# Hybrid DeltaNet and dilated-attention block: one attention clump per step, and weights split anew for each token half

## The chip, the cores and the metric

The kernel runs on one core of a Trainium2 chip. The time is the device time of one execution in microseconds, taken as the median of several runs. Before the change it is 2402.37 us (three runs, 2398.69 to 2404.38). The engines are named as the profile names them: PE (TensorE; PEld are its weight loads), DVE (VectorE), ACT (ScalarE), POOL (GpSimd) and SP (SyncE), which here issues nearly all DMAs.

## The reference, cut to what matters

One decoder layer on 2048 tokens with 1024 channels, all in float32:

```python
h = rms_norm(x, norm_w)
proj = h @ w_in                                   # 1024 x 9224
(dn_qkv, dn_z, dn_b, dn_a, swa_q, swa_k, swa_v, swa_z, gates) = split(proj)
# A: gated DeltaNet, 4 heads: causal conv, silu, l2 norm, chunked delta rule, norm, silu gate
y_dn = o_dn @ w_branch_dn
# B: three groups (window, dilation) = (128,1), (512,4), (2048,16), 4 heads of 128 each:
sq, sk = partial_rope(rms_norm(swa_q)), partial_rope(rms_norm(swa_k))
o_g, lse_g = dilated_window_attention(sq[g], sk[g], sv[g])      # causal, dilated, softmax
o_swa = sum(softmax(lse) * o_g) * silu(swa_z)
y_swa = o_swa @ w_branch_swa
merged = sigmoid(g_dn) * y_dn + sigmoid(g_swa) * y_swa
x = x + merged @ w_out
```

## The kernel before, in words

Float32 products are made of three matmuls on split operands: a high part, cast by a copy on ACT, and a low part, raw minus high, by a subtraction on DVE or POOL (high x high, high x low, low x high).

The projections to q, k and v of branch B (and the two small DeltaNet columns) come first. The 2048 tokens stand in two halves of 1024, called p = 0 and p = 1. In each half a **first unit** makes the values of group 2 straight from x while x is normalised and split, and eight **units** follow. A unit multiplies 1024 tokens by 512 columns with Winograd's form of Strassen's scheme: seven products (the table `PROD`) on quarter operands and their sums S1 to S4 (of x) and T1 to T4 (of weights). Those of x are made once per half (`x_sums`, `x_put`). For a half of p = 0 the weights of each product are loaded raw (`w_load`), summed on DVE (`w_sums`, line 262), copied to the high part on ACT (`w_high`, line 283), and subtracted to the low part (`w_low`, line 290; T2, T3 and T4 on POOL, the others on DVE). Each split weight is then written to a scratch in DRAM (`park`, line 296), and the units of p = 1 read it back (`w_ahead`, line 311) in place of the raw one.

The order on PE, DVE, ACT and POOL is that of the program text; SP's order is the scheduler's. The program spreads work by **hooks**: after every six matmuls `hook()` counts one tick and emits whatever has come due; `at(delay, fn)` puts a function so many ticks ahead. So a delay sets where an instruction stands in its engine's queue, and an instruction that waits there holds all behind it.

**Attention** of a head and group is cut into items of 128 queries. An item runs through: load of q, k and v (`a_load`, lines 565, 566), transposes of q and k (`a_trans`, line 572) with their split into kq on ACT and DVE (579, 580; 576 for group 2), score (`a_score`, lines 590 to 592, or 587) with mask and minimum on DVE (594) and exp on ACT (598), transposes of p (`a_ptrans`, 605) with a copy on ACT (607), and the product with the values (`a_pv`, 613, 614), copied out on DVE (616) and written to scratch (619). One step of `att_loop` has three phases, each at a hook of its own: p's transposes; the score; then the values' product and the next item's transposes. A step takes four hooks in the first half and three in the second. What is left runs in the background of the units that follow.

After the attention projections come 36 **column units** (`cunits`, lines 717 to 719): 128 columns by 2048 tokens in four blocks, for gates and the DeltaNet's k, q and v. The first three are gates; then `open_dn` waits until attention is done and starts the chain of decay matrices E (`e_chain`: a load of gcb, a mask on POOL at line 850, `diff` on DVE at line 857, an exp on ACT). The k block's convolution runs on DVE (lines 823, 827, 832) and its result kT is transposed on PE (883). A scan over chunks, the branch products and the output projection follow; the change leaves them alone.

In the first unit each group of 128 tokens is read twice: by rows (`x_nat`, tile xt, one buffer) for the statistic (`x_stat`) and a diagonal matrix (`x_diag`, 149), and by channels (`x_chan`) for the values; a matmul with the diagonal (153) spreads the scale over the partitions. `x_plan` sets the ticks of all of these.

## Time and profile before

| | |
|---|---|
| median of the runs | 2402.37 us |
| the profiled execution | 2406.0 us, span 2404.2 us |
| PE busy | 2317.2 us, 96% of the span |
| DVE, ACT, POOL busy | 1345.1, 914.8, 886.5 us |
| granted TensorE clock, mean | 0.986 |
| HBM read, written | 263.45 MB, 185.89 MB |
| first unit of p = 0 | about 0 to 70 us |
| units of p = 0 | about 75 to 484 us |
| first unit of p = 1 | about 484 to 556 us |
| units of p = 1 | about 556 to 1015 us |
| column units | from about 1016 us |

PE is busy nearly all the time, so what matters are the gaps on PE and the stretches at a lower clock. A row of the waits gives the waiting instruction, whom it waited for, the sum in us, how often, and the longest.

### The profile page before, as it was taken

The page shows a single profiled execution, that of the slowest core. Times are in us where ns is not written, and L with a number is a line of the kernel's source. Part 1 is how long each engine was busy: PE and PEld are TensorE (multiplying, and loading weights), DVE is VectorE, ACT ScalarE, POOL GpSimd, SP SyncE. Part 2 cuts the span into 40 slices and gives each one's busy share as a digit, 9 for nine tenths or more (in the row PEclk, how much of TensorE's full clock was granted, in tenths as well). Part 3 has the DMA queues.
Part 4 walks back from the last instruction along what each step waited for, and adds up shares of the span by engine and source line. Part 5 has one row for each costly group of instructions (what it writes and reads, how often), then busy time and mean ns, then how long its engine had stood idle before and what let it go on. Part 6 is the DMA issues. An engine that isn't in the chain of part 4 may idle for free.

```text
span 2404.2 us, 43315 instructions
## 1 busy us (share of the span) xinstructions
PE 2317.2 (96%) x15218; PEld 2092.4 (87%) x15218; DVE 1345.1 (56%) x2854; ACT 914.8 (38%) x2941; POOL 886.5 (37%) x1330
## 2 busy tenths in 40 slices
PE   8999999989999999899999999999999999999999
PEld 7998998989999999877778888888888878889998
DVE  6465566675445545443877775999344433344431
ACT  5245455663324435433666662111233313111110
POOL 5263254575403303310845661102233222433441
PEclk9999999989999999999999999999999999999999
DMA  9988888877787787763445443222667645555442
GB/s 308 328 258 266 274 269 247 252 218 235 230 251 235 244 269 221 242 185 93 129 129 133 123 105 120 71 74 71 191 201 208 189 143 158 152 178 163 146 139 76
DMA packets 525968, 452.22 MB, mean 188 GB/s; under 512 B 66168, under 2 KB 490424, under 8 KB 523320
## 3 DMA queue, kind: packets, MB, share of 16 engines
q1 hardware_dynamic: 525464, 449.39, 61.4%
q8 instruction: 121, 1.98, 0.3%
q14 instruction: 95, 0.78, 0.1%
q10 hardware_dynamic: 288, 0.07, 0.0%
HBM read 263.45 MB, written 185.89 MB: 187 GB/s over the span
## 4 chain that ended last, share of the span: by engine, by line
PE 68%; DMA 10%; DVE 6%; issue 5%; POOL 5%; ACT 4%; SPq 1%; POOLq 0%; DVEq 0%; ACTq 0%
PE mm L422 17%; PE mm L717 9%; PE mm L718 9%; PE mm L719 9%; DMA qk<-qks 2%; PE mm L1247 2%; PE mm L1249 2%; PE mm L1248 2%; PE mm L1230 2%; PE mm L1232 2%; PE mm L1231 2%; DMA oscr<-ol 2%; PE tp L572 1%; DMA oc<-oscr 1%; PE po L614 1%
## 5 line engine op out<-in xcount | busy, mean ns | idle before, releaser
L717 PE MATMUL mm<-hh,w 128*128 128x512 f32 x1152 | 464.1, 403 | 5.2 <-DVE gt L1142 3.0
L719 PE MATMUL mm<-hh,w 128*128 128x512 f32 x1152 | 458.2, 398 | 0.0
L718 PE MATMUL mm<-hl,w 128*128 128x512 f32 x1152 | 457.9, 398 | 0.0
L422 PE MATMUL mm<-w,hh 128*128 128x256 f32 x1792 | 353.6, 294 | 5.0 <-ACT ab L548 4.5
L422 PEld LDWEIGHTS mm<-w,hh 128*128 128x128 f32 x1792 | 278.9, 192 | 5.4 <-ACT ab L548 4.7
L422 PE MATMUL mm<-hh 128*128 128x256 f32 x896 | 271.4, 303 | 0.0
L717 PEld LDWEIGHTS mm<-hh,w 128*128 128x128 f32 x1152 | 220.7, 192 | 51.3 <-DVE gt L1142 3.4
L719 PEld LDWEIGHTS mm<-hh,w 128*128 128x128 f32 x1152 | 217.3, 189 | 46.9
L422 PE MATMUL mm<-w,hl 128*128 128x256 f32 x896 | 254.6, 284 | 0.0
L718 PEld LDWEIGHTS mm<-hl,w 128*128 128x128 f32 x1152 | 217.9, 189 | 41.9
L422 PE MATMUL mm<-hl,hh 128*128 128x256 f32 x896 | 253.7, 283 | 0.3 <-POOL hl L290 0.3
L422 PE MATMUL mm<-hh,hl 128*128 128x256 f32 x896 | 253.7, 283 | 0.0
L88 POOL TENSOR_TENSOR w<-raw,w 128x512 fp32r<-128x512 f32 x70 | 102.5, 1466 | 385.0 <-ACT w L87 382.1
L422 PEld LDWEIGHTS mm<-hl,hh 128*128 128x128 f32 x896 | 171.9, 192 | 0.5 <-POOL hl L290 0.5
L422 PEld LDWEIGHTS mm<-hh 128*128 128x128 f32 x896 | 171.9, 192 | 0.0
L422 PEld LDWEIGHTS mm<-w,hl 128*128 128x128 f32 x896 | 171.1, 191 | 0.0
L422 PEld LDWEIGHTS mm<-hh,hl 128*128 128x128 f32 x896 | 171.1, 191 | 0.0
L357 POOL TENSOR_SCALAR st<-st 128x4 f32<-128x4 f32 x96 | 21.8, 228 | 404.5 <-ACT junk L356 402.9
L598 ACT ACTIVATE p<-sc,ol 128x128 f32<-128x128 f32 (+1 forms) x192 | 81.8, 426 | 214.5 <-DVE ol L594 214.2
L594 DVE CUSTOM_DVE_ANT_0 sc<-sc,mask 128x128 f32<-128x128 f32 (+1 forms) x192 | 71.6, 373 | 163.2 <-PE sc L592 58.8
L1230 PE MATMUL mm<-oh,hh 128*128 128x256 f32 x512 | 143.8, 281 | 2.8 <-DVE gt L1234 2.1
L1232 PE MATMUL mm<-oh,hl 128*128 128x256 f32 x512 | 142.9, 279 | 0.0
(299 smaller groups left out, 5507.2 us busy)
## 6 DMA issues: line engine op xcount, KB each, us to landing
wdr<-w SPq DMA_DIRECT2D x56, 512.0 KB, 4.2
w<-wdr SPq DMA_DIRECT2D x56, 512.0 KB, 5.1
qk<-qks SPq DMA_DIRECT2D x212, 128.0 KB, 3.5
qks<-rec SPq DMA_DIRECT2D x96, 256.0 KB, 2.5
raw<-in_w_in_dram SPq DMA_DIRECT2D x70, 256.0 KB, 3.3
gscr<-gt SPq DMA_DIRECT2D x64, 256.0 KB, 2.5
gt<-gscr SPq DMA_DIRECT2D x64, 256.0 KB, 3.5
wdr<-hh SPq DMA_DIRECT2D x28, 512.0 KB, 4.3
```

Of the source, the lines that this page charges most:

```text
L88: eng.tensor_tensor(out=l, in0=raw, in1=h.bitcast(F32), op=ALU.subtract)
L422: mm = lambda x, y, **kw: nc.tensor.matmul(o, x, y, skip_group_check=True, **kw)
L594: nc.vector.tensor_tensor_reduce(out=sc[:, 256 + lo:256 + hi], in0=sc[:, lo:hi], in1=self.mask[:, slot * P + lo:slot * P + hi], scalar=3e3 ...
L598: nc.scalar.activation(p[:, lo:hi], sc[:, 256 + lo:256 + hi], AF.Exp, bias=ol[:, 128:129], scale=-1.0, accum_out=ol[:, 129:130])
L717: nc.tensor.matmul(pr, wh[:, k, :], a, start=(k == 0), stop=False)
L718: nc.tensor.matmul(pr, wh[:, k, :], b, start=False, stop=False)
L719: nc.tensor.matmul(pr, wl[:, k, :], a, start=False, stop=(k == KT - 1))
L1230: nc.tensor.matmul(o, self.wbh[:, k, ms], oh[:, k, :], start=(k == b * 4), stop=False)
L1231: nc.tensor.matmul(o, self.wbh[:, k, ms], ol[:, k, :], start=False, stop=False)
L1232: nc.tensor.matmul(o, self.wbl[:, k, ms], oh[:, k, :], start=False, stop=(k == b * 4 + 3))
L1247: nc.tensor.matmul(pr, mh[:, k, cs], self.woh[:, k, hs], start=(k == 0), stop=False)
L1248: nc.tensor.matmul(pr, mh[:, k, cs], self.wol[:, k, hs], start=False, stop=False)
```

## The change

It does these things. (1) Attention's three phases become one: at each step one clump of score, transposes of q and k, transposes of p and values' product, each for another item; loads go out three steps ahead, the exp, the low part of kq and the copy of the output one hook later; a unit's items begin two steps later, and qk, v and ol get a buffer or two more. In the background of the column units a step takes two hooks and not three. (2) Split weights are no longer written to DRAM: the units of p = 1 load raw weights and make sums and splits as those of p = 0 do. (3) In both first units the weights for the first two products are spread over some hooks, sums of x are made six ticks earlier and in three parts, and the rows of x, their statistic and diagonal come earlier. (4) The first two column units' weights are loaded and split before the last attention unit ends, and their blocks are interleaved. (5) The first piece of the E chain waits ten hooks after its load and not four.

```diff
-        self.wdr = [[self.scratch(f"wdr{j}{x}", [P, 1024]) for x in range(2)] for j in range(56)]
...
-        if u != "f":
-            def park():
-                for x, a in enumerate((h, l)):
-                    self.nc.sync.dma_start(dr(self.wdr[7 * self.pair[u] + PROD_I[name]][x], 0, [[1024, P], [256, 4], [1, 256]]),
-                                           a.bitcast(F32))
-            self.at(2, park)
 
     def w_ahead(self, gi):
         if gi >= 120:
             if gi == 120:
                 self.c_load(0)
+                self.c_load(1)
+                self.at(6, lambda: (self.c_part(0, 0), self.c_part(0, 1)))
             elif gi == 121:
-                self.c_split(0)
+                self.at(1, lambda: (self.c_part(1, 0), self.c_part(1, 1)))
             return
         u, i = self.where(gi)
-        if u != "f" and self.seq[u][0]:
-            h, l = self.W[gi] = tuple(a[:, :, :256] for a in self.ring[gi % 4])
-            for x, a in enumerate((h, l)):
-                self.nc.sync.dma_start(a.bitcast(F32), dr(self.wdr[7 * self.pair[u] + i][x], 0, [[1024, P], [256, 4], [1, 256]]))
-            return
...
-        nxt = u + 1 if not self.seq[u + 1][0] else "f"
-        if i == 5:
+        nxt = "f" if u == 7 else u + 1
+        if nxt == len(self.seq):
+            pass
+        elif i == 5:
             self.w_load(nxt, "B11")
             self.w_load(nxt, "B12")
...
             if p or idx > 1:
-                on(early - 18, lambda m=m: self.x_stat(m))
-                on(early - 14, lambda m=m: self.x_diag(m))
+                on(early - 20, lambda m=m, idx=idx: (self.x_stat(m), self.x_nat(m + 1) if idx < 7 else None))
+                on(early - 15, lambda m=m: self.x_diag(m))
             if p:
-                on(early - 23, lambda m=m: self.x_nat(m))
+                if idx == 0:
+                    on(-29, lambda m=m: self.x_nat(m))
...
             if idx % 2:
-                on(t + 2, lambda m=m: self.x_sums(m))
-                on(t + 6, lambda m=m: self.x_put(m, "S4"))
-                on(t + 9, lambda m=m: self.x_put(m, "S3"))
+                t0 = t + 2 if p and idx == 1 else t - 4
+                on(t0, lambda m=m: self.x_sums(m, 0))
+                on(t0 + 2, lambda m=m: (self.x_put(m, "S1"), self.x_sums(m, 1)))
+                on(t0 + 3, lambda m=m: (self.x_put(m, "S2"), self.x_sums(m, 2)))
+                on(t0 + 5, lambda m=m: self.x_put(m, "S4"))
+                on(t0 + 7, lambda m=m: self.x_put(m, "S3"))
...
             if n == 13:
-                if p:
-                    self.w_ahead(64)
-                    self.w_ahead(65)
-                else:
-                    for c in (4, 5):
-                        self.w_sums(c)
-                        self.w_high(c)
-                        self.w_low(c, nc.vector)
+                g1 = g0 + 4
+                self.w_high(g1)
+                self.at(2, lambda: (self.w_low(g1, nc.vector), self.w_sums(g1 + 1)))
+                self.at(5, lambda: self.w_high(g1 + 1))
+                self.at(7, lambda: self.w_low(g1 + 1))
...
-    def att_loop(self, ph):
+    def att_loop(self):
         if self.att_on:
-            self.att_slots(self.step, ph)
-            if ph == 2:
-                self.step += 1
-            self.at(1 if self.fast else (1, 2, 1)[ph], lambda: self.att_loop((ph + 1) % 3))
+            self.att_step()
+            self.at(3 if self.fast else 4, self.att_loop)
...
-            nc.vector.tensor_tensor(out=l, in0=src, in1=h.bitcast(F32), op=ALU.subtract)
+            self.at(1, lambda: nc.vector.tensor_tensor(out=l, in0=src, in1=h.bitcast(F32), op=ALU.subtract))
...
-            at = max(step + 6, self.att[-1]["at"] + 1) if self.att else step + 6
+            at = max(step + 8, self.att[-1]["at"] + 1) if self.att else step + 8
...
-    def att_slots(self, step, which):
...
+    def att_step(self):
+        step = self.step
+        self.step += 1
+        at = {step - a["at"]: a for a in self.att}
+        if -3 in at:
+            self.a_load(at[-3])
+        for d, fn in ((1, self.a_score), (0, self.a_trans), (2, self.a_ptrans), (3, self.a_pv)):
+            a = at.get(d)
+            if a and (d == 0 or not a["pre"]):
+                fn(a)
...
+        order = [(0, 2), (1, 2), (0, 0), (1, 0), (0, 1), (0, 3), (1, 1), (1, 3)]
+        order += [(u, n) for u in range(2, len(fns)) for n in range(NB)]
+        for u, n in order:
...
-    def e_chain(self, h, period, n=0):
+    def e_chain(self, h, period, n=0, wait=4):
...
-        self.at(4, mask)
-        self.at(5, diff)
-        self.at(7, expo)
+        self.at(wait, mask)
+        self.at(wait + 1, diff)
+        self.at(wait + 3, expo)
         if n + 1 < NB:
             self.at(period, lambda: self.e_chain(h, period, n + 1))
...
-            self.e_chain(0, 7)
+            self.e_chain(0, 7, wait=10)
```

How the instructions stand. First PE in a unit of the first half, one attention step before (mm are the unit's matmuls; po, tp and sc are attention's PSUM tiles):

```order
L613 MATMUL po<-v,pT 128x128
L614 MATMUL po<-v,pT 128x128
L572 MATMUL tp<-ident,qk 128x128 x2
L422 MATMUL mm<-w_224,hh 128x256
...
L605 MATMUL tp<-ident,p 128x128
L422 MATMUL mm<-w_224,hh 128x256
...
L590 MATMUL sc<-kq 128x256
L591 MATMUL sc<-kq 128x256
L592 MATMUL sc<-kq 128x256
```

and in the changed kernel, where lines have other numbers:

```order
L583 MATMUL sc<-kq 128x256
L584 MATMUL sc<-kq 128x256
L585 MATMUL sc<-kq 128x256
L565 MATMUL tp<-ident,qk 128x128 x2
L598 MATMUL tp<-ident,p 128x128
L606 MATMUL po<-v,pT 128x128
L607 MATMUL po<-v,pT 128x128
L414 MATMUL mm<-hh 128x256
```

The three groups, which stood six or twelve matmuls apart, now follow one another, and 24 matmuls lie between one clump and the next (18 in the second half).

Next SP in the second half, before (qk, v, oscr are attention's transfers, wdr the scratch weights):

```order
L565 DMA qk<-qks_83 128x256
L566 DMA v<-vs_92 128x128
L311 DMA hh<-wdr_113 128x4x256
L619 DMA oscr<-ol 128x130
L344 DMA vs_91<-rec 128x2x256
L565 DMA qk<-qks_83 128x256
L311 DMA hl<-wdr_114 128x4x256
L619 DMA oscr<-ol 128x130
```

and now:

```order
L614 DMA oscr<-ol 128x130
L255 DMA wr<-in_w_in_dram 128x4x128
L558 DMA qk<-qks_86 128x256
L559 DMA v<-vs_92 128x128
L614 DMA oscr<-ol 128x130
L255 DMA wr<-in_w_in_dram 128x4x128
```

The two reads of a split weight, for each of seven products, have given way to loads of raw quarters (eight of 128 columns for a unit of q and k, four of 256 for one of v). SP's queue has 1388 rows and had 1605.

Last DVE at the first k blocks, before (acc and kT are the convolution, E the decay matrices):

```order
L815 MEMSET xr 128x3
L823 TENSOR_SCALAR acc<-mm,cw 128x512
L827 SCALAR_TENSOR_TENSOR acc<-xr,cw,acc 128x512 x3
L857 SCALAR_TENSOR_TENSOR E<-gcb,ngc 128x128 x4
L832 SCALAR_TENSOR_TENSOR kT<-kT,acc 128x512
```

and now:

```order
L803 MEMSET xr 128x3
L811 TENSOR_SCALAR acc<-mm,cw 128x512
L815 SCALAR_TENSOR_TENSOR acc<-xr,cw,acc 128x512 x3
L820 SCALAR_TENSOR_TENSOR kT<-kT,acc 128x512
L805 COPY xr<-xr 128x3
L811 TENSOR_SCALAR acc<-mm,cw 128x512
L815 SCALAR_TENSOR_TENSOR acc<-xr,cw,acc 128x512 x3
L845 SCALAR_TENSOR_TENSOR E<-gcb,ngc 128x128 x8
L820 SCALAR_TENSOR_TENSOR kT<-kT,acc 128x512
```

The first four E instructions stood ahead of the first kT; now eight, of two pieces of the chain, stand ahead of the second.

More of the change, by code (lines that the diff above doesn't have):

```diff
@@ L33 @@
         ("S1", "c", True, "T1"), ("A22", "b", False, "T4"), ("S4", "c", False, "B22"))
-PROD_I = {p[3]: i for i, p in enumerate(PROD)}
 C_DN = 0
@@ L502, in f_start @@
         self.x_plan(self.tick, 0)
-        self.at(30, lambda: [self.w_load(0, n) for n in ("B11", "B12", "B22", "B21")])
     def first_unit(self, p):
@@ L507, in first_unit @@
         g0 = 60 * p
+        u = 8 * p
         if p:
@@ L510, in first_unit @@
             self.w_ahead(63)
+            self.at(40, lambda: (self.w_load(u, "B11"), self.w_load(u, "B12")))
+            self.at(44, lambda: self.w_load(u, "B22"))
+            self.at(54, lambda: self.w_load(u, "B21"))
+        else:
+            self.at(30, lambda: [self.w_load(u, n) for n in ("B11", "B12", "B22", "B21")])
         ms = range(8 * p, 8 * p + 8)
@@ L615, in a_pv, with out @@
         ol = a["ol"]
-        nc.vector.tensor_copy(ol[:, :P], po[:, :P])
         row = G * H * 130
         off, st = ((128 * u, 1), (512 * (u % 4) + u // 4, 4), (u, 16))[g]
-        nc.sync.dma_start(dr(self.oscr, off * row + (g * H + a["h"]) * 130, [[st * row, P], [1, 130]]), ol)
+        def out():
+            nc.vector.tensor_copy(ol[:, :P], po[:, :P])
+            nc.sync.dma_start(dr(self.oscr, off * row + (g * H + a["h"]) * 130, [[st * row, P], [1, 130]]), ol)
+        self.at(1, out)
     def att_add(self, h, g, items, step):
         for u, has, pre in items:
-            at = max(step + 6, self.att[-1]["at"] + 1) if self.att else step + 6
+            at = max(step + 8, self.att[-1]["at"] + 1) if self.att else step + 8
             self.aslot = 1 - self.aslot
@@ L641, in att_ready @@
                 self.att_add(h, g, [(7, False, True)] + [(t, True, False) for t in range(8, 16)], self.step)
-    def att_slots(self, step, which):
-        for a in self.att:
-            d = step - a["at"]
-            if "qk" not in a and (d == 0 or (d == -2 and which == 1)):
-                self.a_load(a)
-            if a["pre"] and not (which == 2 and d == 0):
-                continue
-            if which == 0 and d == 2:
-                self.a_ptrans(a)
-            elif which == 1 and d == 1:
-                self.a_score(a)
-            elif which == 2 and d == 2:
-                self.a_pv(a)
-            elif which == 2 and d == 0:
-                self.a_trans(a)
+    def att_step(self):
[8 more added lines that the diff above has]
+                fn(a)
         self.att = [a for a in self.att if step - a["at"] < 4]
@@ L672, in att_background, with go @@
     def att_background(self):
-        def go(which):
-            if not self.att:
-                return
-            self.att_slots(self.step, which)
-            if which == 2:
-                self.step += 1
-            self.at(1, lambda: go((which + 1) % 3))
-        self.at(1, lambda: go(0))
+        def go():
+            if self.att:
+                self.att_step()
+                self.at(2, go)
+        self.at(1, go)
     def c_load(self, u):
@@ L699, in c_part @@
         self.split(self.craw[u][j], wh[:, 4 * j:4 * j + 4, :], wl[:, 4 * j:4 * j + 4, :], self.nc.gpsimd)
[L701 to L703 removed]
     def cunits(self, fns, pre, tail):
         nc = self.nc
[L707 to L708 removed]
+        order = [(0, 2), (1, 2), (0, 0), (1, 0), (0, 1), (0, 3), (1, 1), (1, 3)]
+        order += [(u, n) for u in range(2, len(fns)) for n in range(NB)]
+        for u, n in order:
+            if n == 0 and u in pre:
                 pre[u]()
+            if u + 1 == len(fns) and n == 2:
+                tail()
             wh, wl = self.c_tile(u)
[L711 to L723 removed]
+            pr = self.ps.tile([P, 512], F32, name="mm", bufs=3)
+            for k in range(KT):
+                a, b = self.hh[:, n, k, :], self.hl[:, n, k, :]
+                nc.tensor.matmul(pr, wh[:, k, :], a, start=(k == 0), stop=False)
+                nc.tensor.matmul(pr, wh[:, k, :], b, start=False, stop=False)
+                nc.tensor.matmul(pr, wl[:, k, :], a, start=False, stop=(k == KT - 1))
+                if k % 2:
+                    self.hook()
+            fns[u](n, pr)
+            if (u, n) == (0, 1):
+                self.c_load(2)
+            if (u, n) == (0, 3) or (u > 1 and n == 0 and u + 1 < len(fns)):
+                if u:
                     self.c_load(u + 1)
[L725 removed]
+                for j in range(2):
+                    self.at(4 * j + (4 if u else 1), lambda j=j, v=u + 1 if u else 2: self.c_part(v, j))
     def flush(self):
@@ L1280, in run @@
         self.seq = [(0, *o) for o in order0] + [(1, *o) for o in order1]
-        self.pair = list(range(8)) + [order0.index(o) for o in order1]
         zc = [C_DNZ + j * P for j in range(4)] + [C_SZ + j * P for j in range(4)]
```

65 lines of the change are left out of this document (22 added, 43 removed).

## The prediction

> **What bounds the kernel now.** I read the page's busy shares and clock row first, then the waits of the matrix engine, then a table of stages, then the order of time inside one attention step.
>
> ```profile
> PE 2317.2 (96%) x15218; PEld 2092.4 (87%) x15218; DVE 1345.1 (56%) x2854; ACT 914.8 (38%) x2941; POOL 886.5 (37%) x1330
> PEclk9999999989999999999999999999999999999999
> ```
>
> PE is the bound. The change adds and takes no matmul, so only PE's idle time (2404.2 - 2317.2 = 87 us) and its slow clock can give anything back. Nearly all of the part that the change can reach lies between 70 and 1150 us:
>
> ```profile
> engine line waited for: us in total, times, longest us
> PE tp L605 <- ACT p L598: 17.5, 17, 2.6
> PE tp L572 <- DMA qk<-qks: 10.7, 7, 4.5
> PE tp L153 <- ACT dg L149: 6.7, 3, 2.6
> PE tp L883 <- DVE kT L832: 4.9, 1, 4.9
> PE mm L422 <- ACT ab L548: 4.5, 1, 4.5
> PE sc L590 <- ACT kq L579: 3.1, 5, 0.7
> PE mm L717 <- DVE gt L1142: 3.0, 1, 3.0
> PE mm L717 <- DVE rec L350: 2.2, 1, 2.2
> PE po L613 <- ACT pT L607: 1.6, 2, 0.9
> PE sc L591 <- DVE kq L580: 1.6, 2, 0.8
> ```
>
> Five of these rows are attention (L605, L572, L590, L613, L591): 34.5 us. The stages:
>
> ```profile
> core 0: us, PE busy (x) PEld busy (x) DVE busy (x) ACT busy (x) POOL busy (x), PEclk, DMA share, GB/s
> 75.00:484.00 409.00, 396.79 (x3257) 390.30 (x3256) 247.57 (x563) 205.09 (x679) 188.09 (x282) 0.98 0.85 268
> 484.00:556.00 72.00, 62.60 (x461) 61.48 (x460) 54.97 (x121) 43.30 (x119) 57.88 (x70) 0.91 0.66 203
> 556.00:1015.00 459.00, 437.56 (x3644) 429.94 (x3643) 217.24 (x700) 187.10 (x779) 125.99 (x272) 0.99 0.79 245
> 1140.00:1150.00 10.00, 5.13 (x15) 3.84 (x14) 6.45 (x10) 4.68 (x14) 3.83 (x4) 0.67 0.40 112
> ```
>
> 75 to 484 is the first token half, which makes its weights; 556 to 1015 is the second, which reads them back. The clock costs too. After the 4.9 us wait the 512-column matmuls start 0.43 us apart, and 0.23 us apart once it recovers:
>
> ```profile
> 1145.42 0.66 PE L883 MATMUL tp<-ident,kT 128*128 128x128 f32 x2 [4.87 <-DVE kT L832]
> 1147.16 0.63 PE L717 MATMUL mm<-hh,w 128*128 128x512 f32 x1
> 1147.59 0.63 PE L718 MATMUL mm<-hl,w 128*128 128x512 f32 x1
> 1151.32 0.39 PE L719 MATMUL mm<-hh,w 128*128 128x512 f32 x1
> 1151.55 0.40 PE L717 MATMUL mm<-hh,w 128*128 128x512 f32 x1
> ```
>
> One minus PEclk, times length, over the four stages: 8.2 + 6.5 + 4.6 + 3.3 = 22.6 us, from which the time in which PE stood still anyway is to be taken off.
>
> **The change, part by part.**
>
> *Attention clump.* One step of the second half before:
>
> ```profile
> 841.73 0.28 PE L592 MATMUL sc<-kq 128*128 128x256 f32 x1
> 843.49 0.38 PE L605 MATMUL tp<-ident,p 128*128 128x128 f32 x2
> 846.87 0.38 PE L605 MATMUL tp<-ident,p 128*128 128x128 f32 x2
> ```
>
> A step lasts 846.87 - 843.49 = 3.4 us. From the end of a score (842.0) to the transposes of its p (843.5) there are 1.5 us. In between lie these:
>
> ```profile
> L594 DVE CUSTOM_DVE_ANT_0 sc<-sc,mask 128x256 f32<-128x256 f32 x108 | 46.5, 430 | 73.2 <-PE sc L592 51.4 <-DMA oscr<-ol 10.0 <-PE tp L572 7.2
> L598 ACT ACTIVATE p<-sc,ol 128x128 f32<-128x128 f32 (+1 forms) x192 | 81.8, 426 | 214.5 <-DVE ol L594 214.2
> ```
>
> 0.43 and 0.43 us, and a read of the accumulator after each: 1.2 us in all, which leaves 0.3 us for any queue. In the clump the order is score, transposes of k and q, transposes of p, values, so the score's result is due one whole step later: about 3.4 us in the second half, where 2.2 are free for the queue, and likewise in the first half, with its longer step. The transposes' results (kq) gain alike. The 17 waits at L605 average 1.0 us and the longest is 2.6, so 1.9 us more room ends nearly all: I keep 2.5 of 17.5, and 1 of the other 6.3 (L590, L613, L591). The loads (L572, 10.7 us) are issued three steps ahead and not a little over two, and start two steps later after a unit; with the scratch weights' transfers gone from SP's queue I keep 2.5. Sum: 34.5 - 6.0 = -28.5 us. Clumping itself changes no matmul's price: the same fp32 and split matmuls run back to back.
>
> *Weights made again.* The second half's eight units lose their reads and gain what the first half does:
>
> ```profile
> w<-wdr SPq DMA_DIRECT2D x56, 512.0 KB, 5.1
> L262 DVE TENSOR_TENSOR wr<-wr 128x1024 f32<-128x1024 f32 x29 | 35.6, 1229 | 0.2
> L290 DVE TENSOR_TENSOR hl<-wr,hh 128x1024 fp32r<-128x1024 f32 x16 | 20.5, 1282 | 0.0
> L290 POOL TENSOR_TENSOR w<-wr,w 128x1024 fp32r<-128x1024 f32 x12 | 28.8, 2400 | 40.4 <-ACT w L283 40.4
> L283 ACT ACTIVATE w<-wr 128x1024 fp32r<-128x1024 f32 (+1 forms) x27 | 28.4, 1052 | 18.3 <-DVE wr L262 18.3
> ```
>
> Per unit four sums and four low parts on DVE, three low parts on POOL, seven copies on ACT. Eight units: 32 x 1.23 + 32 x 1.25 = 79 us DVE, 24 x 2.40 = 58 us POOL, 56 x 1.05 = 59 us ACT. Over the 459 us DVE goes from 47% to 64%, ACT from 41% to 54%, POOL from 27% to 40%. The first half stands at 61%, 50% and 46% already and idles PE 12.2 us in 409. So this work hides beside PE, and what shows is that it delays a mask, an exp or a kq. By the rows: at the least nothing, at the most the first half's own rate, 12.2 x 459/409 = 13.7 us. With the wider step I take +6.
>
> A row speaks against taking nothing:
>
> ```profile
> L364 DVE SCALAR_TENSOR_TENSOR rec<-rec,st,wqk x288: 335/346/2499, 146.7 to 1022.6; 128x128 f32<-128x128 f32 x144
> ```
>
> An instruction of 346 ns once took 2499, 2.15 us more, about a low part on POOL. The Trainium skill (SBUF — State Buffer, "SBUF: two separate sides") says why that would be: DVE instructions with two SBUF inputs and GpSimd instructions that read SBUF take one port pair in turn, whole instructions at a time. By that rule all 24 POOL low parts are chances for such a hold; it is the first rival below. The median shows that holds are rare so far.
>
> *Entry to unit 0* (4.5 us, L422 behind L548): the sums and splits of weights 4 and 5 no longer stand in one block on DVE and ACT in front of the copies that free PSUM. I keep 0.5: -4.0.
>
> *Column of x, second half* (6.7 us, L153): the natural rows' load, the statistic and the diagonal are each due earlier, from load to use 17 hooks and not 12. A hook is six matmuls, and 396.79 us for 3257 of them (75 to 484) make 0.12 us each, so 0.7 us a hook: 3.5 us more against waits of at most 2.6. The stage is dense (DVE 76%, POOL 80%), so I keep 1.5: -5.2.
>
> *Start of the column units* (L717, 3.0 + 2.2 us): unit 1's weights are ready, and the blocks that need restored operands come later. But the rows name DVE, whose queue holds the same beta and decay arithmetic. I take -1.5; ends 0 and -5.2.
>
> *First E chain* (4.9 us, L883): the first diff now stands behind the second k block's convolution, so it no longer holds the first kT. But the longer wait reaches only the first piece of the chain (the call for the second passes no wait, so 4 holds), and there is one gcb buffer, which the first diff frees. DVE's order now has eight E instructions in a row ahead of the second kT:
>
> ```profile
> gcb<-gcscr SPq DMA_DIRECT2D x16, 512.0 KB, 4.8
> L850 POOL TENSOR_TENSOR gcb<-gcb,cmask 128x512 f32<-128x512 f32 x16 | 20.8, 1301 | 102.2 <-DMA gcb<-gcscr 100.0 <-DVE acc L827 2.3
> L823 DVE TENSOR_SCALAR acc<-mm,cw 128x512 f32<-128x512 f32 x32 | 23.7, 740 | 0.3 <-ACT xr L819 0.3
> L827 DVE SCALAR_TENSOR_TENSOR acc<-xr,cw,acc 128x512 f32<-128x512 f32 x144 | 122.2, 849 | 18.1 <-ACT acc L825 13.1
> L857 DVE SCALAR_TENSOR_TENSOR E<-gcb,ngc 128x128 f32<-128x128 f32 x64 | 25.3, 455 | 18.6 <-POOL gcb L850 18.6
> L832 DVE SCALAR_TENSOR_TENSOR kT<-kT,acc 128x512 f32<-128x512 f32 x16 | 11.0, 688 | 10.1 <-ACT kT L831 10.1
> ```
>
> From the unit's start, with hooks of six matmuls (6 x 0.23 = 1.38 us): the second block ends at 8 hooks (11.0 us), convolution 0.74 + 3 x 0.85 (14.3), four E (16.1), load (20.9), mask (22.2), four E (24.0), kT (24.7). Its transposes are due at 15 hooks, 20.7 us, some 21.5 with the first block's transposes. So 3.2 us of waiting moves to the second kT; I keep 3.5: -1.4. Bounds: -4.9, if the order of loads is kinder, and nothing.
>
> *Clock.* Of the 22.6 us at most, the waits kept (2.5 + 1 + 2.5 + 0.5 + 1.5 + 3.7 + 3.5, against 55.8 listed) and the added 6 hold over a third, and part fell in standing time: -9, between -3 and -18. The Trainium skill (TensorE: Matmul & The Clock Gate, "What's actually happening") lets the clock fall to half only after an idle window of about 3.4 us. By that rule only the two waits of 4.5 us that I end would give clock back, about 2 us each by the rows of the recovery, and the sum would come out 5 us higher. The trace disagrees so far: from 484 to 556 no listed wait is over 2.6 us and PEclk is 0.91.
>
> *Sum*: -28.5 + 6 - 4.0 - 5.2 - 1.5 - 1.4 - 9 = -43.6 us. The profiled execution took 2406.0 us (span 2404.2), so 2362.4; it lies 3.6 us above the median of the runs, 2402.4, on whose scale I forecast **2359 us**, with 2348 to 2370 as this case's own range.
>
> **Rivals.**
>
> *The remade weights hold the attention chain: slower, 2427.* Every one of the 56 weight groups of the second half puts a 1.23 us sum, a 1.05 us copy or a 2.40 us low part in front of a mask, an exp or a kq. If each costs PE one wait of the mean size at L605 (17.5/17 = 1.0 us), that is 56 us in place of my 6, and the second half's attention gains (most of its 459 - 437.6 = 21.4 us idle, say 18) are not made: -43.6 - 6 + 18 + 56 = +24. It decides from 31.6/56 = 0.56 us a group. For it: DVE at 64% and the L364 row. Against it: the first half does all this with 12.2 us idle, at a narrower step. The port rule quoted above would have it through POOL alone: 24 holds of up to 2.15 us, 52 us. Chance 0.09.
>
> *The wait changes its name: 2377.* The masks already wait for results on their way out (L594, 10.0 us on oscr<-ol in its wide form); the output copy now comes a hook later, against one more ol buffer. If attention keeps half of its gain (+14) and the clock too (+4.5), 2359 + 18.5. For it: SP still issues every load and store in order. Against: the scratch traffic that filled the queues (DMA 0.85 and 0.79 busy) goes. Chance 0.25.
>
> *All listed waits go: 2329.* 34.5 + 4.5 + 6.7 + 5.2 + 4.9 = 55.8 us, 18 of clock, nothing added: 2406.0 - 73.8 - 3.6. Against it: the E chain above. Chance 0.13.
>
> *Nothing to be told, 0.05*: 0.2% either way is 2397.6 to 2407.2, about what a measurement of this kernel can tell from no change; it needs the first rival at about half strength. That the change doesn't do what it says is not open: in the order the clumps stand, SP has 217 rows fewer, and the second half's sums are there.
>
> **How the numbers follow.** Forecast 0.48, name change 0.25, all gone 0.13, nothing 0.05, slower 0.09. Faster by over 0.2% is 0.48 + 0.25 + 0.13 = 0.86, same 0.05, slower 0.09. The range takes the forecast and the name change with the bounds of attention and clock, and the upper part of "all gone": 2330 to 2392, which leaves out some 0.2.
>
> **What would show it.** Right: waits at the transposes of p under 5 us in all; qk waits under 4; weight-group waits of L422 still near 1 us; DVE in the second half near 64%; the DMA share in both halves well under 0.7; no wait at unit 0's entry; one wait of 3 to 4 us at the kT transposes, now at the second block. Wrong: PE idle of over 25 us in the second half with DVE or POOL named (the first rival), or masks that wait for oscr over 30 us (the second). PE's busy time and matmul count must stay; if they move, the sum has the wrong base.

## The result, and the profile after

| | before | changed |
|---|---|---|
| median of the runs | 2402.5 us (2398.7 to 2404.4) | 2360.9 us (2357.0 to 2361.1) |
| ratio | | 0.9825, 95% interval 0.9808 to 0.9842 |
| profiled execution, span | 2404.2 us | 2358.9 us |
| DMA, HBM read and written | 263.45 and 185.89 MB | 221.51 and 127.17 MB |

The changed kernel is 1.75% faster, and the forecast of 2359 us was 2 us off. The parts of the sum fared less well than the sum.

The busy shares and the clock row of the changed kernel's page:

```profile
PE 2297.6 (97%) x15216; PEld 2083.8 (88%) x15216; DVE 1424.4 (60%) x2917; ACT 950.9 (40%) x2996; POOL 957.2 (41%) x1355
PEclk8999999999999999999999999999999999999999
```

DVE has gained 79 us and POOL 71, PE's matmuls are the same (two records are missing), and the slice of the clock row near 500 us that read 8 reads 9; the first one, at the start, reads 8 now. PE idles 61.3 us of the span, where it idled 87.

The waits of PE in the changed kernel (waiting instruction, whom it waited for, sum in us, times, longest). Rows that lie wholly in the first 70 us or behind 1150 us are left out, and two of 0.3 us at the units' weights; of the first two rows, 6.7 and 4.2 us lie between 70 and 1150 us:

```profile
PE tp L151 <- ACT dg L147: 14.9, 8, 3.6
PE tp L871 <- DVE kT L820: 7.0, 4, 4.2
PE sc L583 <- ACT p L591: 5.4, 8, 2.2
PE sc L580 <- ACT p L591: 4.6, 8, 1.0
PE tp L598 <- DVE kq L573: 3.2, 4, 1.2
PE sc L584 <- DVE kq L573: 2.7, 3, 1.4
PE tp L598 <- DVE wr L158: 2.4, 1, 2.4
PE po L607 <- DVE ol L613: 1.2, 3, 0.7
PE sc L580 <- DVE kqT L569: 0.8, 1, 0.8
PE tp L598 <- ACT p L591: 0.2, 1, 0.2
```

The rows of before read 17.5 us at the transposes of p and 10.7 at the loads of q and k, and the list of before has two more attention rows beside the five in the prediction:

```profile
PE tp L605 <- DVE kq L580: 0.9, 2, 0.6
PE po L614 <- ACT pT L607: 0.3, 1, 0.3
```

Now the transposes of p wait 0.2 us for the exp (and 5.6 for others: 3.2 for kq, 2.4 for a scaling of x on DVE), and the loads are not in the list at all. In their place stand rows that were not there: scores that wait for the exp of the item before, 10.0 us in all. Attention's rows together went from 35.7 to 20.5 us. The wait at unit 0's entry (4.5 us) and those at the column units' start (5.2 us) are gone.

The stages of the changed kernel, columns as in the table of before:

```profile
75.00:484.00 409.00, 404.36 (x3398) 402.49 (x3397) 270.78 (x608) 216.11 (x737) 204.84 (x312) 1.00 0.46 137
484.00:556.00 72.00, 65.35 (x517) 64.55 (x517) 55.35 (x93) 37.97 (x90) 54.61 (x52) 0.95 0.64 195
556.00:1015.00 459.00, 442.00 (x3582) 427.98 (x3581) 292.62 (x804) 231.26 (x840) 194.80 (x306) 1.00 0.56 165
```

The second half's DVE stands at 292.62/459 = 64%, as forecast; the DMA share fell from 0.85 and 0.79 to 0.46 and 0.56. These windows are cut at fixed times, and the kernels are shifted against each other by up to 38 us there. So I also cut by place in the program. For each pair of successive matmuls I take the time from start to start, less what that matmul takes when nothing holds it (0.229 us for 512 columns, 0.1185 for 256; these bases sum to 2234 us in every kernel). What is left is PE's lost time, in us, with waits and slow clock in it:

```
stage            before   changed   difference
first unit, p=0    22.3      20.6      -1.7
units 0 to 7       31.6      10.4     -21.2
first unit, p=1    12.8      10.5      -2.3
units 8 to 15      36.8      26.6     -10.2
column units 0-2   10.1       6.9      -3.2
DeltaNet units     18.1      15.1      -3.0
the rest           32.9      29.4      -3.5
total             164.6     119.4     -45.2
```

Split by kind over the whole program, gaps of over 0.2 us went from 102.9 to 70.0 us, the excess of matmuls in slow stretches (stretches at a lower clock) from 21.8 to 11.9, and the small rest from 39.8 to 37.5.

### The profile page after: what moved, and what is told of

It reads as the page before. It is cut to its first block, busy times and chain, and to the rows that moved or that the text cites. A ratio compares the mean times of both kernels' runs of the same rounds, so it can differ in the third digit from the quotient of the medians.

```text
span 2358.9 us, 43166 instructions
## 1 busy us (share of the span) xinstructions
PE 2297.6 (97%) x15216; PEld 2083.8 (88%) x15216; DVE 1424.4 (60%) x2917; ACT 950.9 (40%) x2996; POOL 957.2 (41%) x1355
## 3 DMA queue, kind: packets, MB, share of 16 engines
HBM read 221.51 MB, written 127.17 MB: 148 GB/s over the span
## 4 chain that ended last, share of the span: by engine, by line
PE 49%; DMA 3%; DVE 3%; POOL 2%; ACT 1%; issue 1%; SPq 0%; POOLq 0%; DVEq 0%; ACTq 0%
PE mm L701 9%; PE mm L702 9%; PE mm L703 9%; PE mm L1237 2%; PE mm L1235 2%; PE mm L1236 2%; PE mm L1218 2%; PE mm L1220 2%; PE mm L1219 2%; DMA gcb<-gcscr 1%; DVE E L845 1%; DVE acc L815 1%; DMA raw<-in_w_out_dram 1%; PE po L1078 1%; PE tp L1072 1%
## 5 line engine op out<-in xcount | busy, mean ns | idle before, releaser
L414 PE MATMUL mm<-w,hh 128*128 128x256 f32 x1792 | 334.2, 286 | 0.3 <-POOL w L289 0.3
L414 PE MATMUL mm<-hh 128*128 128x256 f32 x896 | 261.4, 292 | 0.0
L1219 PE MATMUL mm<-ol,hh 128*128 128x256 f32 x512 | 142.9, 279 | 0.0
L815 DVE SCALAR_TENSOR_TENSOR acc<-xr,cw,acc 128x512 f32<-128x512 f32 x144 | 120.7, 838 | 18.2 <-ACT acc L813 13.3
```

The lines of the kernel that those rows point to most:

```text
L414: mm = lambda x, y, **kw: nc.tensor.matmul(o, x, y, skip_group_check=True, **kw)
L815: nc.vector.scalar_tensor_tensor(out=acc, in0=xr[:, j:j + 512], scalar=w[:, j:j + 1], in1=acc, op0=ALU.mult, op1=ALU.add)
L1219: nc.tensor.matmul(o, self.wbh[:, k, ms], ol[:, k, :], start=False, stop=False)
```

## The experiments

All ratios are to the kernel before, on the same chip and in the same job. The kernel before took 2399.5 to 2402.5 us in the different jobs, so runs of different jobs are compared by their ratios: 0.001 is 2.4 us, and an interval reaches some 0.001 to 0.002 to either side. Five runs undo one part of the change each, and one undoes two. The earlier sums of x and the longer wait of the first E piece were not undone alone.

### Undoing the clump

```diff
-((1, score), (0, trans), (2, ptrans), (3, pv)) in one hook, every 4 (3) hooks
-exp, kq's low part, ol's copy: self.at(1, ...)
+three phases at hooks of their own; exp, low part and copy at once
-load at d == -3; bufs qk 4, v 8, ol 4
+load at d == 0 and d == -2 (phase 1); bufs qk 3, v 6, ol 3
+a unit's items begin at step + 6 (8 in the change); background: three hooks a step (2)
```

> The change without its attention clump: three phases a step again, the mask, the exp, the low parts and the output copies emitted at once, the loads two steps and a little ahead, buffers 3, 6 and 3; both halves still make their weights. In the changed kernel the attention lines wait 18.2 us in all (10.0 of it scores that wait for the last exp). Theory 1 (the clump gave the score's result a step, and it is what makes the remade weights free): the waits at the p-transposes return, 15 to 25 us, the scores' waits for the exp go under 2, attention 25 to 35 us in all, time 2370 to 2390, ratio to before 0.987 to 0.995. Theory 2 (the remade weights hold the attention chain, and only the clump covers them): p-transposes over 40 us, time over 2395. Theory 3 (the parked weights' transfers were the cause of all attention waits): attention stays under 20 us, time 2356 to 2366. For the loads' own waits (10.7 us before, none now): over 6 us if the clump's longer lead ended them, under 2 if the end of the parked weights' traffic did.

Measured: 2401.6 us median of ten runs (2396.6 to 2404.2), ratio 1.0003 (0.9989 to 1.0017). Everything that the change gave is gone. The largest of PE's waits in its units 8 to 15:

```profile
PE tp L600 <- ACT p L593: 12.9, 19, 1.7
PE sc L585 <- ACT kq L574: 4.3, 3, 2.0
PE sc L586 <- DVE kq L575: 3.7, 1, 3.7
PE tp L567 <- DMA qk<-qks: 2.7, 2, 2.5
```

The waits at the transposes of p are back (15.8 us over the whole span), and so are those for kq. This is theory 1 in its rows; the time went beyond its range, to where theory 2 had put it, but without theory 2's sign of over 40 us at the transposes of p. Of the loads' 10.7 us, 2.7 came back, between the two marks set for them (the next two runs take this up).

A likely reason why so small a reordering does so much is seen in DVE's and ACT's own waits. Before:

```profile
DVE ol L616 <- PE po L614: 100.7, 113, 4.1
DVE kq L580 <- ACT kq L579: 86.7, 128, 2.5
ACT p L598 <- DVE ol L594: 214.2, 155, 6.3
```

With the clump undone and the weights remade:

```profile
DVE kq L575 <- ACT kq L574: 94.7, 130, 4.0
DVE ol L611 <- PE po L609: 88.6, 110, 2.1
ACT p L593 <- DVE ol L589: 186.3, 149, 3.2
```

Changed:

```profile
DVE kq L573 <- ACT kq L572: 25.6, 37, 2.1
DVE ol L613 <- PE po L607: 4.5, 6, 1.7
ACT p L591 <- DVE ol L587: 34.8, 28, 4.3
```

In the old order, the copy of ol, kq's low part and the exp stood in their queues before their inputs were there, 402 us in sum before and 370 here, and all other work of DVE and ACT (sums and splits of weights among it) stood behind them. One hook later, the inputs have mostly come (65 us). The clump is a wider step for PE, but also this: engines that no longer stand waiting at the head of their queues. How much of the time belongs to this was not shown: the run undoes the order, the hook more, the earlier loads, the buffers and the background's step together, and no run takes them apart.

### Undoing the remade weights

```diff
-second half: w_load, w_sums, w_high, w_low as in the first
+first half parks h and l in DRAM (wdr); second half reads them back
```

> The change without its remade weights: the first half parks its split weights in DRAM and the second half reads them back, as before; the clump and all the rest stay. DMA share should be back near 0.8 in both halves and VectorE near 47% in the second. Theory 1 (the clump's lead ended the loads' waits, and the remade weights cost PE little): no load waits over 2 us, attention 12 to 20 us, time 2352 to 2362, so the removal of the parking is worth nothing. Theory 2 (the parked weights' transfers held the loads and the results on their way out): waits for qk of 5 to 11 us, or masks that wait for oscr over 10 us, time 2364 to 2376. Theory 3 (the remade weights take from the attention chain): the scores' waits for the exp fall from 10.0 to under 5 us and the time to 2348 to 2354.

Measured: 2358.2 us (2355.8 to 2359.7), ratio 0.9825 (0.9806 to 0.9844). The change without its remade weights is as fast as with them. Its stages, and its masks' waits on DVE for results that have not left yet:

```profile
75.00:484.00 409.00, 401.04 (x3357) 398.52 (x3356) 267.44 (x607) 215.13 (x734) 202.66 (x308) 0.99 0.88 280
556.00:1015.00 459.00, 446.18 (x3651) 434.32 (x3651) 226.94 (x765) 187.69 (x799) 134.59 (x292) 1.00 0.82 251
```

```profile
DVE sc L599 <- DMA oscr<-ol: 72.8, 30, 4.5
```

The traffic is back (DMA 0.88 and 0.82). It holds masks for 72.8 us, 25.4 in the change, and yet the loads of q and k wait only 1.5 us on PE: the clump's lead covers them. Theory 1's time holds; its 12 to 20 us of attention waits too, with 12.3 us of scores waiting for the exp. One of theory 2's signs, masks that wait over 10 us, is there without its time.

### Undoing both, with the small edits kept

The diff is that of the two runs above together.

> The fourth cell of a two by two: neither clump nor remade weights, only the small edits (first units, x columns, start of the column units, first E wait). Idle and slow time of PE over its start-to-start base in the second half so far: 34 us without either (kernel before), 22 with the clump alone, 55 with the remade weights alone, 30 with both. Theory 1 (the two parts interact: the remade weights cost the old three-phase chain some 20 us and the clump 9): this cell shows 30 to 38 us in the second half, and a time of 2380 to 2390 (the remade weights alone 10 to 20 us slower than this, at 2401.6). Rival (the remade weights cost nothing, and the slow time of the clump's undoing comes from the small edits): second half 48 to 58 us, time 2397 to 2405.

Measured: 2400.1 us (2396.5 to 2405.3), ratio 0.9992 (0.9980 to 1.0004). Theory 1's time is wrong: without clump and remade weights the small edits give at most 0.2%, not 12 to 22 us. The waits show where their gain went:

```profile
PE tp L612 <- ACT p L605: 15.5, 20, 2.9
PE tp L891 <- DVE kT L840: 11.1, 4, 8.0
PE tp L579 <- DMA qk<-qks: 10.1, 6, 3.3
```

The loads wait as before; the longest kT wait is 8.0 us where it was 4.9. The loads' waits are thus nearly ended by either part: 10.1 us with neither, 2.7 without the traffic, 1.5 with the clump, none with both. So the two by two is this, in medians and ratios:

```
                    weights read back    weights made again
three phases         2400.1 (0.9992)      2401.6 (1.0003)
clump                2358.2 (0.9825)      2360.9 (0.9825)
```

By ratio the clump is worth 40 us in one column and 43 in the other, the remade weights nothing that can be told in either row (2.6 us and none, within the intervals). By stage, in PE's lost time as defined above ("both again" is a second run of the changed kernel):

```
stage            neither   weights   clump   both   both again
units 0 to 7       23.7      13.8     15.2   10.4     11.1
first unit, p=1    15.5      12.0     12.0   10.5      9.2
units 8 to 15      48.9      54.5     20.9   26.6     23.9
DeltaNet units     20.4      21.6     16.1   15.1     14.9
```

Each column is one profiled execution, and kernels that share a stage's code differ there by up to some 12 us (units 8 to 15 of the kernel before: 36.8, with neither part: 48.9), so only the large differences count. In units 8 to 15 the clump takes 28 us away with either kind of weights. The remade weights read 3 to 6 us dearer there, and 4 to 10 us cheaper in units 0 to 7, where nothing is parked any more; both lie within that spread. The rival's numbers came in (48.9 us, 2400.1). Whether the 12 us above the kernel before are spread or the work of the small edits, as the rival has it, is not decided: neither kernel has a second profile.

### Undoing the entry to unit 0

```diff
 if n == 13 (first half only):
-    w_high(4); at 2: w_low(4), w_sums(5); at 5: w_high(5); at 7: w_low(5)
+    for c in (4, 5): w_sums(c); w_high(c); w_low(c) on DVE
```

> The change with one place put back: in the first first-unit the sums and splits of weights 4 and 5 stand in one block on VectorE and ScalarE again. My theory: a wait of 4 to 5 us returns at the first matmuls of unit 0 and the clock drops after it, time 2364 to 2369. Rival (the other order of the sums of x had already ended it): no wait over 1.5 us there, time 2358 to 2362.

Measured: 2363.1 us (2359.4 to 2366.1), ratio 0.9841 (0.9818 to 0.9863).

```profile
PE mm L414 <- ACT ab L549: 3.8, 1, 3.8
```

The wait returns, 3.8 us of it, and a stretch of slow clock after it (75.95 to 79.37 us in the clock's records). The row bears my theory out. The time lies just under its range; by ratio it is 3.8 us above the change, and the intervals overlap.

### Undoing the start of the column units

```diff
-order (0,2),(1,2),(0,0),(1,0),(0,1),(0,3),(1,1),(1,3); units 0 and 1 loaded ahead
+unit 0: 2,0,1,3; then unit 1; unit 1 loaded after unit 0's first block
```

> The change with the start of the column units put back: unit 1's weights are loaded and split after the first block of unit 0, and the units follow one another. My prediction's reading (VectorE's beta and decay arithmetic holds the blocks, so the new order is worth 1.5 us of 5.2): waits there of 1 to 2 us, time 2360 to 2364. Rival (the order itself decides: a block's PSUM is freed late and unit 1's weights are late): waits of 4 to 6 us at the first blocks, time 2364 to 2370.

Measured: 2360.9 us (2357.4 to 2364.3), ratio 0.9837 (0.9816 to 0.9857). No wait at the first blocks appears. Neither reading is right: with the clump in place the old order waits for nothing there, and the ratio's 2.9 us above the change lie within the intervals. In the kernels with three phases it mattered: with the old start (before) the first blocks wait 3.0 us for gt and 2.2 for rec, with the new one (clump undone, both undone) 2.5 for rec alone. So this edit ends the one wait, and with the clump neither stands.

### The mask into p

```diff
-tensor_tensor_reduce(out=sc[:, 256 + lo:256 + hi], in0=sc[:, lo:hi], ...)
-at(1): activation(p, sc[:, 256 + lo:256 + hi], Exp, ...)
+tensor_tensor_reduce(out=p[:, lo:hi], in0=sc[:, lo:hi], ...)
+at(1): activation(p, p, Exp, ...)
```

> The changed kernel with one size of the score's life altered: the mask writes its result into p in SBUF instead of the second half of the score's PSUM bank, and the exp works in place in p. So the one sc bank is free after the mask, a hook and an exp earlier than now. Theory 1 (the scores' new waits, 5.4 + 4.6 us, come from the single sc bank that the delayed exp holds): waits of scores for the exp under 2 us, second half's waits down by 6 to 9 us, time 2350 to 2356. Rival (the exp itself is late on ScalarE's queue, and the wait only changes its name): p-transposes wait for the exp 5 to 10 us where they wait 0.2 now, time 2358 to 2363.

Measured: 2354.6 us (2353.2 to 2356.3), ratio 0.9816 (0.9798 to 0.9834). The kernel before took 2399.5 us in this job, so by ratio this is 2 us better than the change, which the intervals can't tell from nothing. Scores that wait for the exp are not in the list any more. The transposes of p wait for it instead, and a score waits for the mask:

```profile
PE tp L598 <- ACT p L591: 3.2, 6, 0.8
PE sc L583 <- DVE ol L588: 0.4, 1, 0.4
```

So the new 10.0 us at the scores came from the clump with one score bank: the next item's score comes a step later, and the exp that is now emitted a hook late must have read the bank. But not all of it went. 3.2 us changed name (the transposes of p), and attention's rows together fell from 20.5 to 16.3 us. In units 8 to 15 the listed waits went from 14.1 to 11.8 us, not down by 6 to 9, and the lost time from 26.6 (23.9 in the second run) to 22.9. Theory 1 is right on the cause of the row, not on its worth.

### The longer E wait for all pieces

```diff
-self.at(period, lambda: self.e_chain(h, period, n + 1))
+self.at(period, lambda: self.e_chain(h, period, n + 1, wait))
```

> The changed kernel with the longer wait passed on to all four pieces of the first E chain, not the first alone. My prediction's reading of the second kT block (the second piece's four E instructions stand ahead of it, since the call for the second piece passes no wait): the 4.2 us wait at the transposes of kT goes under 1.5, all kT waits from 7.0 to under 4.5, time 2355 to 2358. Rival (the wait at the second block comes from the convolution itself, or the E instructions arrive late for the q blocks instead): kT stays over 6 us or a wait of 2 us or more appears at the products of q and k, time 2359 to 2363.

DVE's order in the changed kernel, around the 4.2 us wait at kT:

```profile
1099.68 1.13 DVE L845 SCALAR_TENSOR_TENSOR E<-gcb,ngc 128x128 f32<-128x128 f32 x4
1107.25 2.12 DVE L845 SCALAR_TENSOR_TENSOR E<-gcb,ngc 128x128 f32<-128x128 f32 x4 [6.43 <-POOL gcb L838]
1109.29 0.68 DVE L820 SCALAR_TENSOR_TENSOR kT<-kT,acc 128x512 f32<-128x512 f32 x1
```

DVE stood 6.43 us for the second piece's mask, with the second kT behind it. With the wait passed on: 2355.2 us (2354.3 to 2355.9), ratio 0.9819 (0.9798 to 0.9840), and

```profile
PE tp L871 <- DVE kT L820: 3.5, 3, 1.5
PE sc L924 <- ACT qT L819: 1.1, 1, 1.1
```

The 4.2 us wait is gone and 1.1 us turns up at a product of q and k. By its row the reading is right; the time, by ratio 1.4 us better than the change, can't be told from it.

### The x column of the second half

```diff
 x_stat, x_diag ahead (hooks), second half
-20, 15      (the change)
+24, 20      (first run)      18, 14 in both halves (second run, as before the change)
 the first load of rows: 29 ahead (the change), 33 (first run), 23 (second run)
```

> The changed kernel with the statistic and the diagonal of the second half's x columns four and five hooks earlier still, so that each diagonal's copy stands on ScalarE ahead of the previous column's split, and not behind it. The profile of the changed kernel has the diagonal done 3.2 us late because the split ahead of it on ScalarE waits for a scaling on VectorE, which waits 3.0 us for the column's load. Theory 1 (that queue order is what holds the ones-by-diagonal product): its waits in the second first-unit fall from 7.1 to under 3 us, time 2355 to 2359. Rival (the natural rows' load into its one buffer is what is late, so an earlier due time moves nothing): 6 to 8 us stay, time 2359 to 2363.

> The change with this part put back: statistic and diagonal of x 18 and 14 hooks ahead, as before, not 20 and 15. My prediction said that the two and one hooks more would end 5.2 of 6.7 us; the profile says that they ended nothing. If the profile is right, the ones-by-diagonal waits of the second first-unit stay within 2 us of 7.1; if the earlier times helped against something that the change made worse, they rise to 10 us or more.

These waits are the row at L151, the matmul with the diagonal. In the changed kernel the first of them looks like this, on DVE and on ACT:

```profile
484.36 2.15 DVE L158 SCALAR_TENSOR_TENSOR wr<-wr,nw,tp 128x128 f32<-128x128 f32 x8 [3.00 <-DMA wr<-in_xcol_dram]
```

```profile
485.52 0.63 ACT L179 ACTIVATE hh<-wr 128x512 fp32r<-128x512 f32 x1 [3.11 <-DVE wr L158]
487.08 0.39 ACT L147 ACTIVATE dg<-ident,xst 128x128 f32<-128x128 f32 x1
```

The diagonal (487.08) stood on ACT behind the split of the column before, that behind a scaling, that behind the column's load. With the statistic four and the diagonal five hooks earlier the ones-by-diagonal waits of this stage vanish (7.4 us in all are left, all in the first half's first unit), as theory 1 had it, but

```profile
PE mm L527 <- ACT ab L543: 3.8, 1, 3.8
```

stands there, and PE loses 8.3 us over its start-to-start base from 484 to 556 us, 10.5 in the change. Time 2357.7 us (2355.8 to 2359.7), ratio 0.9829 (0.9810 to 0.9848): not to be told from the change. With the old times: 5.3 us of these waits, 2356.9 us in a single run. That says little: in the second run of the unaltered change the row reads 4.0 us and the wait at L527 is there too with 1.1, and runs that leave this stage alone (the mask into p, the longer E wait) have 4.1 and 3.0 beside 2.7 at L527. The stage loses some 7 to 10 us whatever the diagonal's time is; that the loads set it was not tried.

### A version that beats both

Three versions on one chip: the changed kernel again, and two that join the mask into p and the longer E wait. The first of these has five ol buffers, the second four and another order in the clump.

```diff
 first:  ol bufs=4 -> bufs=5
 second: (score, trans, ptrans, pv) -> (score, trans, pv, ptrans)
```

> The changed kernel itself, unaltered, as the neighbour of the two versions sent with it on the same chip: 2357 to 2363, ratio 0.981 to 0.985.

> A version meant to beat both: the mask into p (alone: 2354.6 against 2360.9 of the change), the longer E wait for all four pieces (2355.2), and five ol buffers for four, since masks wait 25 us for results on their way out. If the gains add (they lie in different stages): 2347 to 2351. If the mask's and the E chain's gains were mostly the spread of the runs: 2353 to 2358. The fifth ol buffer should take the masks' waits for oscr from 25 to under 12 us on VectorE; if these waits are on PE's path, the second half's waits fall by 3 us or more, otherwise by under 1.

> The mask into p and the longer E wait for all pieces as in the other version, four ol buffers, and in the clump the values of the step before ahead of the transposes of p, which gives the exp and the kq low part two more float32 matmuls of time (some 0.45 us). If the exp's remaining waits at the transposes of p (3.2 us) are short ones of under 0.5 us, they fall to under 2 and the time to 2346 to 2350; if the values then wait for the last copy of pT instead, that row appears with 2 us or more and the time is 2349 to 2354.

Measured: the change 2360.7 us (0.9824, 0.9810 to 0.9837); with five ol buffers **2343.0 us** (2339.3 to 2345.6; 0.9746, 0.9732 to 0.9759); with the other order 2353.3 us (0.9793, 0.9779 to 0.9806).

The first is 17.7 us faster than the change, on the same chip. By ratio the single gains of mask and E wait were 2.2 and 1.4 us, both within their intervals, and the second version, which has both and four buffers, gains 7.4. So some 10 us of the 17.7 go with the fifth buffer and the unaltered order; the buffer was not run alone. A gain from it was expected only if the masks' waits for results on their way out lie on PE's path. The row of masks waiting for oscr (25.4 us in the change, 28.2 with the other order) is gone with five buffers. The page and the transposes of p:

```profile
PE 2291.0 (98%) x15216; PEld 2079.1 (89%) x15216; DVE 1425.4 (61%) x2917; ACT 956.8 (41%) x2996; POOL 963.8 (41%) x1355
```

```profile
PE tp L598 <- ACT p L591: 2.5, 5, 0.8
```

By place in the program, units 8 to 15 lose 16.0 us here, 26.6 and 23.9 in two runs of the change and 22.9 with the mask into p alone. With the other order the exp's row at the transposes of p falls to 1.6 us, but scores wait 4.4 us for kq; whether it gains anything over the two edits can't be told from these ratios.

## Why the prediction was right, and where it was not

- **What bounds the kernel**: right. PE's matmuls are the base, and the gain is lost time around them. But I had taken the page's busy time for that base and said that it must stay, and it fell from 2317.2 to 2297.6 us. The base from start to start did stay (2234 us): the page's busy time also holds the slow matmuls and holds too short to show as idle. So idle time (87 to 61 us) and the slow excess (9.9 us) are some 36 of the span's 45 us.
- **Attention clump, -28.5 us of waits**: the mechanism was right and its side effect missed. The transposes' waits for the exp went from 17.5 to 0.2 and the loads' from 10.7 to nothing, both better than the 2.5 us that I kept for each. But "1 of the other 6.3" failed: with one score bank and an exp emitted a hook late, scores wait 10.0 us for the exp, and rows that name kq and ol wait 7.9; all waits at the transposes of p are 5.8 us, over my mark of 5. Attention's rows gave 15.2 us, not 28.5. Against that, the clump alone moves the time by 40 to 43 us, more than its waits and its share of the clock: it also carries a gain that I had booked elsewhere (the column units' start), and some that I had not booked.
- **Weights made again, +6**: DVE's 64% was right. In time the sum is nothing that can be told, none by ratio with the clump and 2.6 us without. The profiles read 3 to 6 us more in units 8 to 15 and, a term that I had not, 4 to 10 us less in units 0 to 7, which no longer park; both are within what executions differ by.
- **Entry to unit 0, -4.0**: right as a wait (4.5 gone, 3.8 back when undone); as time 3.8 us by ratio, not clear of the spread.
- **Column of x, -5.2**: wrong. The change's waits in that stretch sum to 6.7 us, as before (4.0 and 1.1 at L527 in its second run). The step that failed is "3.5 us more against waits of at most 2.6": the diagonal was not late by its due time but by its place on ACT, behind a split that waits for a load.
- **Column units' start, -1.5**: all 5.2 us went. Without the clump the edit is worth 2.7 of them, with it no wait: undone, none returns. That DVE's beta and decay arithmetic would hold the blocks anyway fell with that.
- **First E chain, -1.4**: right in mechanism, with the eight E instructions ahead of the second kT; 4.2 us stand there where I kept 3.5, so 0.7 us of the wait went and not 1.4. Without the clump the same edit leaves a wait of 8.0.
- **Clock, -9**: right, 21.8 to 11.9 us of slow excess, -9.9. The Trainium skill's rule (TensorE: Matmul & The Clock Gate, "What's actually happening") would have given back about 4 us for the two long waits; the trace disagrees with it as a threshold on single gaps, as the last section shows.
- **The rivals**: "the remade weights hold the attention chain" needed 56 us; even with the old chain the remade weights read 6 us in the second half, so it falls with and without the clump. Single holds are there, as the port rule of the Trainium skill (SBUF — State Buffer, "SBUF: two separate sides") would have it: the 346 ns scaling took 2531 ns at the longest, 2499 before, about a low part on POOL. But it took over 1 us eight times now and seven before, with twice the weights' low parts on POOL (50 and 25), and no row of PE's waits names it. "The wait changes its name" happened in part, through the score's bank (10.0 us). Its sign, masks that wait for oscr over 30 us, stayed below (25.4), but was a poor one: in all its forms that row already read 32.4 us before, and 72.8 in a run as fast as the change. The version with the fifth ol buffer suggests that these waits cost something too.

So the sum was right by compensation, which is luck: attention's rows gave 13 us less than forecast and the x column 5 less, while the column units' start gave 4 more, the remade weights cost nothing where I had 6, and some 10 us of lost time that no row of my list held went too (45.2 in all, of which rows and clock account for 35.5). The parts that I costed as separate (entry, column, start, E: 12.1 us) are worth at most 0.2% without the clump.

## What to carry to other kernels

An instruction that is put in its engine's queue before its input is there holds all work behind it. Emitting such instructions one slot later, in one clump with the rest of their step, with earlier loads and a buffer or two more, here gave some 40 us; what each of these gave alone was not measured. The 79 us of added VectorE work cost nothing that could be told, with the clump or without it. A result that is consumed a step later also holds its buffer a step longer: look at once for the buffer that becomes the next wait (here the score's PSUM bank and the ol tiles: the version that treats both, with one E delay, is 17.7 us faster). And when several edits meet in one change, each wait that it ends should be tested against the largest edit alone before it is credited to the small one beside it.

## What the hardware showed that I had not expected

The granted clock falls in pieces: in the profile's clock records every slow stretch in the six profiles that I compared (before, changed, clump undone, both undone, mask into p, five ol buffers) lasts 3.41 us or a multiple of it (6.83, 10.24, and 13.65 at the start of two), but for the piece that the end of the program cuts off, and the clock in it is half. Between 40 and 2300 us, all 16 gaps on PE of over 3.23 us (start to start, less the base) have such a stretch beginning within them or within 4 us after, and so have 21 of the 32 gaps between 2.1 and 3.23 us; the mark lies at the longest gap that has none. So gaps well under one piece can be enough, and in these profiles a wait of 2.5 us is likelier than not to cost more than itself: 3.41 us at half clock is 1.7 us of work.

VectorE's scaling of q and k (288 instructions of one shape) took 425 ns on average before and 451 in the change, 26 ns or 6% more: some 7.5 us in all, which no row of PE's waits shows. Twice the low parts on POOL (26 and 24 of 2.40 us) are not shown to be the cause: with the clump undone and the same low parts it took 435 ns, with both undone 432, and with only the weights read back 423. Its sums of weights took 1228 ns before, 1265 in the change and 1268 with the weights read back.
